# Deferred attention work behind every second score tile, and modulation rows loaded from GpSimd's queue

## The chip, the cores and the metric

The kernel runs on one core of a Trainium2 chip. The metric is the device time of one execution in microseconds (us); lower is better. A profile is one further execution, recorded by the hardware profiler. Its engines are PE (TensorE: PE is the matmul, PEld the weight load beside it), DVE (VectorE), ACT (ScalarE), POOL (GpSimd) and SP (SyncE, which here only issues transfers); SPq and POOLq are the instruction queues of SP and GpSimd. L344 is line 344 of the kernel in question.

## The reference

One block of a diffusion backbone works on 512 latent tokens and 256 context tokens of width 1024. The inputs are modulated, one combined projection feeds two kinds of attention, both are gated and merged, and a mixture of 16 experts follows. Cut to what is computed:

```python
mod = silu(c) @ w_ada + b_ada                 # w_ada: 1024 x 6144
sh1, sc1, g1, sh2, sc2, g2 = split(mod, 6)
mod_c = silu(c_ctx) @ w_ada + b_ada           # its first two parts
h, hc = x * (1 + sc1) + sh1, ctx * (1 + sc1c) + sh1c
p, pc = h @ w_in, hc @ w_in                   # 1024 x 4000
# latent attention: c_q, c_kv by rms_norm, then w_uq, w_ukv; 8 heads
o_mla = softmax(q_mla k_mla^T * scale) v_mla
# differential attention: 4 heads, two score maps each
w = softmax(q1 k1^T * s) - lam * softmax(q2 k2^T * s)
o_diff = rms_norm(w dv, g_subln) * (1 - lambda_init)
y = gate_a * (o_mla @ w_o_mla) + gate_b * (o_diff @ w_o_diff)
x = layer_norm(alpha * x + g1 * (y @ w_out))
x = layer_norm(alpha * x + g2 * ec_moe(x * (1 + sc2) + sh2))
# ec_moe: each of 16 experts takes its 64 best tokens, SwiGLU of 1024
```

The first third of the modulation, sh1 and sc1, is wanted at once, since the projections read x and ctx modulated by it. The other four parts, g1, sh2, sc2 and g2, are wanted only behind the attention.

## The kernel before

Everything up to the experts is written for a framework whose scheduler fixes, when the kernel is built, the order of the instructions on each engine; an engine then runs its own list in order, waits included. Code order counts in that, and the rings of buffers count: a tile with bufs=3 is a ring of three, and a fourth user waits until the first buffer's last reader is done.

**Start.** The parts sh1 and sc1 are worked out by quarters of the columns. For each quarter, SP loads two blocks of w_ada (tile wa, L222 and L223, 128x2048 each), a quarter of x and ctx (xq, L226 and L227), and a page of w_in (wraw, L196). PE multiplies the w_ada blocks by the activated condition (tile tp, L237), DVE copies the result (ms, L240), PE transposes it, and DVE adds it up to the scales and shifts (scv, shv). Then x is transposed on PE, modulated on DVE (xtmp), and split into a rounded part (xlh, xch on ACT) and a rest (xll, xcl on GpSimd, L78). A product of two such pairs is three matmuls (L82 to L84), into the accumulators acc. The key projection of the differential attention runs in step with the quarters.

**Projections.** chunk() and gates() go through the columns of w_in. A weight page wraw is split like x into whi (ACT, L75) and wlo (DVE, L78). There are six pages of this kind.

**Modulation rows.** The other four parts of the modulation need 32 loads of 128x1024 floats (512 KB) of w_ada, L344. DVE multiplies each by one column of the condition and adds the eight of a part up (L346 for the first of eight, L348 for the others). After eight, mod_sum() sums over the partitions on PE (L358), loads two rows of b_ada (L359) and adds them on DVE (L360) into rm. The tile is wa2 (wa in the profile), a ring of N_WA = 3 that the b_ada rows share. The calls of mod_chunk() are set by a table of places, MOD_AT: eight within the value projection, twelve in gates(0), twelve in gates(1). What the eighth row leaves to do, mod_sum(), stands in a list, late, and is run by the next call. All these loads are issued by SP, in whose queue the pages of w_in, w_ukv and w_uq stand too.

**Attention.** A score tile is one block of 128 queries against 768 keys: scores() on PE (tile sc, L653), the maximum on DVE (L642), the exponential on ACT (L643). The transposes of the weights (tpb, L661) and the value products (av, L841 in the latent attention) are put off: defer() queues them with a cost and the earliest slot, and fill() runs as many of them as a share of the queued cost allows. fill() is called after each score tile, four calls in a half head, and each counts as one slot. A value product of one 128-key block (kc) is one deferred piece of cost 0.43 (differential) or 0.86 (latent, two heads at once).

**Experts.** From about 560 us on the order is written out by hand; the weights of the experts stream through the same pages, and through others that come free behind the attention.

## Time and profile before

| | us |
|---|---|
| median of three runs | 1046.89 |
| lowest and highest of them | 1044.27 and 1050.75 |
| the profiled execution | 1044.37 |
| its span in the profile | 1042.6 |
| PE busy | 980.1 (94%) |
| DVE busy | 447.2 (43%) |
| ACT busy | 278.3 (27%) |
| POOL busy | 173.4 (17%) |
| bytes moved | 266.98 MB, mean 256 GB/s |

The span is what the profile shows of the execution; the time holds 1.77 us more around it. PE is busy nearly throughout, but a busy PE may still be at different work per microsecond, and a short wait of PE in one stage can come from an engine that is mostly idle. So the stretches have to be read one by one: start (0 to 46 us), projections (to 150), gates with latent projections and modulation rows (to 262), differential attention (to 330), latent attention (to 460), output projection and router (to 560), experts (from there).

### The profile page before, as it was taken

The page shows a single profiled execution, that of the slowest core. Times are in us where ns is not written, and L with a number is a line of the kernel's source. Part 1 is how long each engine was busy: PE and PEld are TensorE (multiplying, and loading weights), DVE is VectorE, ACT ScalarE, POOL GpSimd, SP SyncE. Part 2 cuts the span into 40 slices and gives each one's busy share as a digit, 9 for nine tenths or more (in the row PEclk, how much of TensorE's full clock was granted, in tenths as well). Part 3 has the DMA queues.
Part 4 walks back from the last instruction along what each step waited for, and adds up shares of the span by engine and source line. Part 5 has one row for each costly group of instructions (what it writes and reads, how often), then busy time and mean ns, then how long its engine had stood idle before and what let it go on. Part 6 is the DMA issues. An engine that isn't in the chain of part 4 may idle for free.

```text
span 1042.6 us, 13825 instructions
## 1 busy us (share of the span) xinstructions
PE 980.1 (94%) x5280; PEld 615.3 (59%) x5280; DVE 447.2 (43%) x871; ACT 278.3 (27%) x556; POOL 173.4 (17%) x176
## 2 busy tenths in 40 slices
PE   6999999999989999999996999999999999999982
PEld 5888977768778777777764443535353534234331
DVE  2382366662678555558473312221313131111227
ACT  1222325224777555544110101010101010010010
POOL 2340020202677322210021400000000000000004
PEclk9999999999999999999998999999999999999997
DMA  9944347752111100038948989999999999999993
GB/s 299 289 157 131 96 119 257 239 189 78 27 35 57 41 1 21 21 99 300 406 161 325 376 303 408 409 409 409 409 408 409 409 409 409 409 409 409 410 371 118
DMA packets 101210, 266.98 MB, mean 256 GB/s; under 512 B 14020, under 2 KB 37528, under 8 KB 101144
## 3 DMA queue, kind: packets, MB, share of 16 engines
q1 hardware_dynamic: 100248, 264.52, 68.2%
q0 software_dynamic: 320, 1.05, 0.3%
q8 instruction: 42, 0.69, 0.3%
q10 hardware_dynamic: 576, 0.52, 0.1%
q14 instruction: 24, 0.20, 0.1%
HBM read 261.47 MB, written 2.10 MB: 253 GB/s over the span
## 4 chain that ended last, share of the span: by engine, by line
PE 70%; DMA 10%; issue 9%; DVE 5%; POOL 2%; ACT 2%; SPq 0%; POOLq 0%; DVEq 0%; ACTq 0%
PE h L1179 15%; PE y L1195 8%; PE mx L1142 6%; PE acc L82 5%; PE acc L84 5%; PE acc L83 5%; DMA wr<-moe_w 5%; PE sc L653 4%; DMA wa<-w_ada 3%; PE tpb L661 3%; PE av L841 3%; PE mx L1208 2%; PE po L84 1%; PE po L83 1%; PE po L82 1%
## 5 line engine op out<-in xcount | busy, mean ns | idle before, releaser
L1179 PE MATMUL h<-wr,xe 128*64 128x512 f32 x1024 | 233.6, 598 | 8.9 <-DMA wr<-moe_w 7.9
L1179 PEld LDWEIGHTS h<-wr,xe 128*64 128x64 f32 x1024 | 68.2, 136 | 163.0 <-issue 106.6
L1195 PE MATMUL y<-wr,hidT 128*64 128x512 f32 x448 | 97.7, 594 | 0.0
L642 DVE TENSOR_REDUCE nm<-sc 128x1 f32<-128x768 f32 x64 | 61.0, 953 | 34.4 <-PE sc L653 33.8
L1182 DVE TENSOR_TENSOR hid<-hid,h 128x512 f32<-128x512 f32 x16 | 11.0, 688 | 147.8 <-PE h L1179 147.8
L1195 PEld LDWEIGHTS y<-wr,hidT 128*64 128x64 f32 x448 | 31.5, 137 | 61.8 <-issue 58.2
L1154 POOL TENSOR_TENSOR oh<-oh,aff 128x512 f32<-128x512 f32 x8 | 8.4, 1048 | 350.2 <-PE mx L1142 350.2
L643 ACT ACTIVATE P<-sc,nm 128x768 f32<-128x768 f32 x64 | 57.6, 901 | 31.8 <-DVE nm L642 22.7
L1142 PE MATMUL mx<-oh,xn 128*128 128x128 f32 x512 | 60.4, 280 | 1.4 <-DVE oh L1132 1.4
L1142 PEld LDWEIGHTS mx<-oh,xn 128*128 128x128 f32 x512 | 59.4, 196 | 2.5 <-issue 1.3
L75 ACT ACTIVATE whi<-wraw 128x1024 fp32r<-128x1024 f32 (+1 forms) x32 | 33.5, 1046 | 100.8 <-DMA wraw<-w_in 76.8
L78 DVE TENSOR_TENSOR wlo<-wraw,whi 128x1024 fp32r<-128x1024 f32 (+1 forms) x32 | 38.7, 1209 | 45.0 <-PE acc L83 29.1
L75 ACT ACTIVATE ye<-y 128x512 fp32r<-128x512 f32 (+2 forms) x17 | 9.7, 572 | 178.1 <-DVE y L1202 98.7
L82 PE MATMUL acc<-xlh,whi 128*128 128x512 f32 x128 | 51.6, 403 | 2.8 <-ACT whi L75 2.0
L1209 DVE TENSOR_TENSOR acc<-acc,mx 128x512 f32<-128x512 f32 x56 | 34.7, 680 | 41.4 <-PE mx L1208 41.4
L1181 ACT ACTIVATE hid<-h 128x512 f32<-128x512 f32 x16 | 9.6, 597 | 154.9 <-PE h L1179 154.9
L83 PE MATMUL acc<-xll,whi 128*128 128x512 f32 x128 | 50.8, 397 | 0.0
L82 PE MATMUL acc<-whi,xlh 128*128 128x512 f32 (+1 forms) x128 | 49.5, 391 | 1.0 <-ACT whi L75 1.0
L84 PE MATMUL acc<-xlh,wlo 128*128 128x512 f32 x128 | 50.0, 398 | 0.0
L1202 DVE SCALAR_TENSOR_TENSOR y<-y,gate,g2b 128x512 f32<-128x512 f32 x14 | 9.9, 754 | 92.6 <-PE y L1195 92.6
L84 PE MATMUL acc<-whi,xll 128*128 128x512 f32 (+1 forms) x128 | 48.7, 381 | 0.5 <-POOL xll L78 0.5
L83 PE MATMUL acc<-wlo,xlh 128*128 128x512 f32 (+1 forms) x128 | 48.8, 381 | 0.2 <-DVE wlo L78 0.2
(341 smaller groups left out, 1704.4 us busy)
## 6 DMA issues: line engine op xcount, KB each, us to landing
wr<-moe_w SPq DMA_DIRECT2D x372, 512.0 KB, 10.2
wa<-w_ada SPq DMA_DIRECT2D x32, 512.0 KB, 4.6
wraw<-w_in SPq DMA_DIRECT2D x28, 512.0 KB, 4.8
wa<-w_ada SPq DMA_DIRECT2D x8, 1024.0 KB, 9.8
wr<-moe_w SPq DMA_DIRECT2D x16, 384.0 KB, 8.4
outraw<-w_out SPq DMA_DIRECT2D x8, 512.0 KB, 11.1
xq<-x SPq DMA_DIRECT2D x4, 512.0 KB, 7.8
q<-q SPq DMA_DIRECT2D x16, 128.0 KB, 2.3
```

The source lines that it names most:

```text
L75: S.activation(hi, src, AF.Copy)
L78: (eng_lo or V).tensor_tensor(lo, src, f(hi), op=OP.subtract)
L82: T.matmul(ps, lh, rh, start=start, stop=False)
L83: T.matmul(ps, lh, rl, start=False, stop=False)
L84: T.matmul(ps, ll, rh, start=False, stop=stop)
L642: V.tensor_reduce(nm, ps[:, :768], axis=AX.X, op=OP.max, negate=True)
L643: S.activation(p, ps[:, :768], AF.Exp, bias=nm, accum_out=z)
L653: T.matmul(ps[:, a:b], l, r[:, a:b], start=i == 0, stop=i == len(passes) - 1)
L1142: T.matmul(pss[hf][:, kk * 128:(kk + 1) * 128], xn[t][:, k * 128:(k + 1) * 128], o[:, t].rearrange("p e s -> p (e s)"), start=t == 0, stop ...
L1179: T.matmul(ph[i][64 * hf:64 * hf + 64, :], xe[:, k, sl], w[:, hf * 512:(hf + 1) * 512], start=k == 0, stop=k == KD - 1)
L1195: T.matmul(py[hf][r0:r0 + 64, :], hT[:, e % 2, fc % 4, fc // 4, :], w[:, hf * 512:(hf + 1) * 512], start=fc == 0, stop=fc == KD - 1)
L1209: V.tensor_tensor(acc[t][:, hs], acc[t][:, hs], ps, op=OP.add)
```

## The change

It does three things. The modulation rows and the b_ada rows are issued by GpSimd instead of SP. mod_chunk() first issues and multiplies its own row and only then runs what the row before it left to do. In the attention, two score tiles are issued together, then their softmaxes, and fill() is called once for the two, with two slots and twice the share of the queued cost; the value products are deferred in threes (differential) or all six at once (latent).

```diff
--- before.py
+++ after.py
@@ -334,14 +334,17 @@
 
     def mod_chunk():
 
-        for fn in late:
+        due = late[:]
+        late.clear()
+        if len(halves) < 4 * KD:
+            mod_part()
+        for fn in due:
             fn()
-        late.clear()
-        if len(halves) == 4 * KD:
-            return
+
+    def mod_part():
         j, k = divmod(len(halves), KD)
         wa = mw.tile([128, D], F32, name="wa2", bufs=N_WA)
-        dma(wa, w_ada[:, k, (2 + j) * D:(3 + j) * D])
+        G.dma_start(wa, w_ada[:, k, (2 + j) * D:(3 + j) * D])
         if k == 0:
             V.tensor_scalar(wa, wa, cs[:, 0, 0:1], None, op0=OP.mult)
         else:
@@ -356,7 +359,7 @@
         bm = mw.tile([128, D], F32, name="wa2", bufs=N_WA)
         for g in (2 * h, 2 * h + 1):
             T.matmul(pm[32 * g:32 * g + 32, :], one2[:, 0:1].to_broadcast([128, 32]), wa[:, (g % 2) * 512:(g % 2) * 512 + 512], start=True, stop=True)
-            dma(bm[32 * g:32 * g + 32, :512], b_ada[4 + 4 * i + g:5 + 4 * i + g].to_broadcast([32, 512]))
+            G.dma_start(bm[32 * g:32 * g + 32, :512], b_ada[4 + 4 * i + g:5 + 4 * i + g].to_broadcast([32, 512]))
         V.tensor_tensor(rm[i][64 * h:64 * h + 64], pm[64 * h:64 * h + 64], bm[64 * h:64 * h + 64, :512], op=OP.add)
 
     def chunk(col, n, cuts, evac, at, nxt):
@@ -512,10 +515,10 @@
             first = turns[turn] = max(first, turns.get(turn, 0))
         later.append((cost, first, fn, key))
 
-    def fill(parts):
-
-        slot[0] += 1
-        budget = sum(w[0] for w in later) / parts
+    def fill(parts, n=2):
+
+        slot[0] += n
+        budget = n * sum(w[0] for w in later) / parts
         i = 0
         while i < len(later) and budget > 0:
             c, first, fn, _ = later[i]
@@ -750,14 +753,15 @@
                     prep_pair(0)
             for t in (2 * half, 2 * half + 1):
                 z1 = wk.tile([128, 1], F32, name="z1", bufs=6)
-                ps_ = []
+                ps_, scs = [], []
                 for m in range(2):
                     q1, q2, k1 = (qk[hd, m, nm] for nm in ("q1", "q2", "k1"))
                     tsl = slice(t * 128, (t + 1) * 128)
-                    sc = scores([(q1[:, tsl], k1), (q2[:, tsl], k1)])
-                    ps_.append(softmax(sc, z1 if m else z0[:, t:t + 1],
+                    scs.append(scores([(q1[:, tsl], k1), (q2[:, tsl], k1)]))
+                for m in range(2):
+                    ps_.append(softmax(scs[m], z1 if m else z0[:, t:t + 1],
                                        wpage("P1", F32, [128, D])[:, :768] if m else p_tile()))
-                    fill(D_PARTS)
+                fill(D_PARTS)
 
                 V.reciprocal(z1, z1)
                 V.scalar_tensor_tensor(z1, z1, nlam, z0[:, t:t + 1], op0=OP.mult, op1=OP.mult)
@@ -780,8 +784,8 @@
                     finish(hd, avs[hd], z0, ("d", hd))
             for j in range(3):
                 defer(0.45, lambda j=j, tr=tr: tr(j), D_TR, ("d", hd), "tr")
-            for kc in range(NK):
-                defer(0.43, lambda kc=kc, pv=pv: pv(kc), D_TR + 1, ("d", hd), "pv")
+            for k0 in range(0, NK, 3):
+                defer(1.3, lambda k0=k0, pv=pv: [pv(kc) for kc in range(k0, k0 + 3)], D_TR + 1, ("d", hd), "pv")
     close_qb()
 
     w_od = A["diff_w_o"][0].rearrange("(k p) n -> p k n", p=128)
@@ -813,18 +817,19 @@
         if h % 2 == 1 and pr + 1 < HEADS // 2:
             prep_pair(pr + 1)
         for half in range(2):
-            ws_ = []
+            ws_, scs = [], []
             for t in (2 * half, 2 * half + 1):
                 tsl = slice(t * 128, (t + 1) * 128)
                 qx, qy = qts[h][0][:96, tsl], qts[h][1][:96, tsl]
                 kx, ky = kt[h % 3][0][:96], kt[h % 3][1][:96]
-                sc = scores([(qx, kx), (qx, ky), (qy, kx)])
+                scs.append(scores([(qx, kx), (qx, ky), (qy, kx)]))
+            for sc in scs:
                 z = wk.tile([128, 1], F32, name="zm", bufs=6)
                 p = softmax(sc, z, p_tile())
                 V.reciprocal(z, z)
                 G.tensor_scalar(p, p, z, 1.0, op0=OP.mult, op1=OP.mult)
                 ws_.append(p)
-                fill(M_PARTS)
+            fill(M_PARTS)
 
             def tr(j, ws_=ws_, h=h, half=half):
                 if j == 0:
@@ -847,8 +852,7 @@
             for j in range(3):
                 defer(0.45, lambda j=j, tr=tr: tr(j), M_TR, None, "tr")
             if h % 2 == 1:
-                for kc in range(NK):
-                    defer(0.86, lambda kc=kc, pv=pv: pv(kc), M_TR + 1, None, "pv")
+                defer(2.6, lambda pv=pv: [pv(kc) for kc in range(NK)], M_TR + 1, None, "pv")
             if half == 1:
                 box = []
                 if h % 2 == 0:
```

(In the attention's lines G is GpSimd, V is DVE, T is PE and S is ACT.)

The order at three places shows what this moves. The first is GpSimd's and DVE's list at the start of the program, before against after; wa_739 and its like are modulation rows, tri is a constant mask, xll and xcl are the rests of x and ctx of the first quarter. GpSimd:

```order
 masks.py:65 MEMSET tri 128x128
+L347 DMA wa_739<-w_ada 128x1024
 masks.py:66 AFFINE_SELECT tri<-tri 128x128
+L347 DMA wa_760<-w_ada 128x1024
+L347 DMA wa_787<-w_ada 128x1024
+L347 DMA wa_808<-w_ada 128x1024
+L347 DMA wa_835<-w_ada 128x1024
 L78 TENSOR_TENSOR xll<-xtmp,xlh 128x512
 L78 TENSOR_TENSOR xcl<-xtmp,xch 128x256
 L78 TENSOR_TENSOR xll<-xtmp,xlh 128x512
 L78 TENSOR_TENSOR xcl<-xtmp,xch 128x256
+L347 DMA wa_856<-w_ada 128x1024
```

Five row loads now stand ahead of the first quarter's rests on GpSimd, and the next behind them. DVE, at the same place, where cs is the condition's columns and vecs a table of biases:

```order
 L169 TENSOR_SCALAR cs<-sg 128x8
+L349 TENSOR_SCALAR wa_739<-wa_739,cs 128x1024
+L351 SCALAR_TENSOR_TENSOR wa_760<-wa_760,cs,wa_739 128x1024
 L240 COPY ms<-tp 128x128
 L183 COPY vecs<-tp 128x68
+L351 SCALAR_TENSOR_TENSOR wa_787<-wa_787,cs,wa_760 128x1024
 L184 TENSOR_SCALAR gsub<-vecs 128x1
 L247 SCALAR_TENSOR_TENSOR scv<-tp,vecs 128x4
```

Two multiplications by rows that are still to be loaded stand ahead of the copy ms of the first quarter, and a third ahead of scv.

The second place is the stretch of gates(0) and the latent projections. SP's list before, where wraw is a page of w_in and wa2 a modulation row:

```order
L196 DMA wraw_1439<-w_in 128x2x512
L344 DMA wa2_1382<-w_ada 128x1024
L344 DMA wa2_1397<-w_ada 128x1024
L196 DMA wraw_1485<-w_in 128x2x512
L344 DMA wa2_1412<-w_ada 128x1024
L344 DMA wa2_1421<-w_ada 128x1024
L466 DMA wukv_1530<-mla_w_ukv 128x1024
L471 DMA wuq_1536<-mla_w_uq 128x768
L344 DMA wa2_1436<-w_ada 128x1024
L344 DMA wa2_1451<-w_ada 128x1024
L471 DMA wuq_1540<-mla_w_uq 128x768
L196 DMA wraw_1740<-w_in 128x2x512
```

SP's list of the change at this place:

```order
L196 DMA wraw_1439<-w_in 128x2x512
L196 DMA wraw_1485<-w_in 128x2x512
L469 DMA wukv_1530<-mla_w_ukv 128x1024
L474 DMA wuq_1536<-mla_w_uq 128x768
L474 DMA wuq_1540<-mla_w_uq 128x768
L196 DMA wraw_1740<-w_in 128x2x512
L196 DMA wraw_1779<-w_in 128x2x512
```

The rows are gone from it, and only weight pages are left. GpSimd's list of the change there, in which qtok is the sum that closes the rotary embedding of the latent queries, and of which the list before had only the qtok lines:

```order
L347 DMA wa2_1436<-w_ada 128x1024
L347 DMA wa2_1451<-w_ada 128x1024
L347 DMA wa2_1460<-w_ada 128x1024
L347 DMA wa2_1475<-w_ada 128x1024
L362 DMA wa2_1479<-b_ada 32x512 x2
L347 DMA wa2_1497<-w_ada 128x1024
L347 DMA wa2_1506<-w_ada 128x1024
L502 TENSOR_TENSOR qtok_1334<-q1t_1601,q2t_1602 128x2x32
L502 TENSOR_TENSOR qtok_1335<-q1t_1601,q2t_1602 128x2x32
L347 DMA wa2_1521<-w_ada 128x1024
L502 TENSOR_TENSOR qtok_1336<-q1t_1619,q2t_1620 128x2x32
```

The rows now stand in line with the qtok sums, which wait for DVE.

The third place is PE in the latent attention. Its list before, where av is a value product (wT holds transposed weights, vm the values), sc a score matmul and tpb a transpose:

```order
L841 MATMUL av<-wT,vm 64x256 x11
L653 MATMUL sc<-K,Q 128x512 x3
L653 MATMUL sc<-K,Q 128x256 x3
L661 MATMUL tpb<-ident,P 128x128 x8
L841 MATMUL av<-wT_3224,vm 64x256
L661 MATMUL tpb<-ident,P 128x128 x4
L841 MATMUL av<-wT_3454,vm 64x256
L653 MATMUL sc<-K,Q 128x512 x3
L653 MATMUL sc<-K,Q 128x256 x3
L841 MATMUL av<-wT_3224,vm 64x256
L841 MATMUL av<-wT_3454,vm 64x256
L841 MATMUL av<-wT_3224,vm 64x256
```

PE's list of the change there:

```order
L664 MATMUL tpb<-ident,P 128x128 x4
L846 MATMUL av<-wT,vm 64x256 x11
L664 MATMUL tpb<-ident,P 128x128 x4
L656 MATMUL sc<-K,Q 128x512 x3
L656 MATMUL sc<-K,Q 128x256 x3
L656 MATMUL sc<-K,Q 128x512 x3
L656 MATMUL sc<-K,Q 128x256 x3
L664 MATMUL tpb<-ident,P 128x128 x8
L846 MATMUL av<-wT_3550,vm 64x256
```

The products, which before were broken up by scores and transposes, now stand in one block, and two score tiles follow each other.

## Rows read from the trace of the kernel before

**Rows 1.** Busy time by stretch, whole span.
```profile
...
core 0: us, PE busy (x) PEld busy (x) DVE busy (x) ACT busy (x) POOL busy (x), PEclk, DMA share, GB/s
2.00:46.00 44.00, 36.63 (x313) 29.89 (x314) 13.77 (x30) 9.05 (x17) 11.85 (x11) 1.00 1.02 323
...
150.00:226.00 76.00, 71.44 (x309) 55.29 (x308) 50.13 (x82) 24.52 (x63) 6.72 (x16) 0.98 0.74 245
...
262.00:330.00 68.00, 62.17 (x379) 52.49 (x377) 50.41 (x86) 50.21 (x108) 47.65 (x36) 1.00 0.14 30
330.00:460.00 130.00, 126.79 (x780) 96.04 (x782) 76.62 (x130) 71.96 (x137) 37.21 (x38) 1.00 0.13 41
...
560.00:1015.00 455.00, 444.72 (x2259) 192.03 (x2257) 108.17 (x213) 48.13 (x94) 21.97 (x20) 1.00 1.00 394
```

**Rows 2.** Who waited for whom on PE, 0 to 62 us: total, times, longest.
```profile
...
PE tp L237 <- DMA wa<-w_ada: 4.2, 2, 4.0
...
PE acc L82 <- ACT whi L75: 1.0, 1, 1.0
```

**Rows 3.** DMA issues of SP in order of time, 10 to 30 us.
```profile
...
18.37 4.46 SPq L223 DMA_DIRECT2D wa<-w_ada  x1
```

**Rows 4.** The chain of waits, whole span: start us, us, what.
```profile
...
22.82 1.94 PE tp L237 x32
...
35.46 3.22 PE tp L237 x64
...
376.77 1.24 PE sc L653 x6
...
382.73 1.05 PE sc L653 x6
...
862.52 10.18 DMA wr<-moe_w
```

**Rows 5.** Instructions on the tile wa, whole span: its loads.
```profile
...
DMA to landing us min/median/max: 2.0/4.6/14.0
```

**Rows 6.** Line 344, 150 to 228 us.
```profile
...
L344 SPq DMA_DIRECT2D wa<-w_ada x23: 327/328/350, 151.1 to 218.4; - x23
...
DMA to landing us min/median/max: 3.5/4.6/5.0
```

**Rows 7.** Line 348, 150 to 228 us: duration ns min/median/max.
```profile
...
L348 DVE SCALAR_TENSOR_TENSOR wa<-wa,cs,wa x21: 1276/1284/1337, 154.8 to 223.6; 128x1024 f32<-128x1024 f32 x21
```

**Rows 8.** The chain of waits, 150 to 232 us.
```profile
...
152.16 4.59 DMA wa<-w_ada
156.84 1.30 DVE wa L348
...
173.52 1.29 DVE wa L348
174.86 1.05 PE tp L358 x4
...
202.84 6.64 DMA wraw<-w_in
```

**Rows 9.** Who waited for whom on PE, 140 to 262 us.
```profile
...
PE acc L82 <- ACT whi L75: 2.0, 1, 2.0
PE tp L358 <- DVE wa L348: 1.5, 1, 1.5
PE acc L82 <- DVE q2t L496: 0.8, 1, 0.8
```

**Rows 10.** Busy time around one wait of PE.
```profile
...
210.70:214.60 3.90, 3.90 (x10) 3.05 (x11) 3.33 (x3) 0.41 (x1) 0.00 (x0) 0.58 0.91 285
```

**Rows 11.** GpSimd in order of time, 560 to 610 us.
```profile
...
565.61 0.76 POOL L1217 DMA_DIRECT2D gb<-ln_g  x1 [20.23 <-issue]
...
571.78 0.59 POOL L1217 DMA_DIRECT2D gb<-ln_g  x1 [1.04 <-PE h L1179]
```

**Rows 12.** Line 1217, whole span: from issue to landing.
```profile
...
DMA to landing us min/median/max: 6.1/6.5/7.8
```

## The prediction

> **What bounds the kernel now.** I read the busy time by stretch first [rows 1]. In every stretch PE is the engine nearest to full, but for two reasons. At the start transfers fill the span: 323 GB/s, and PE is busy 36.6 of 44 us. In the experts the DMA share is 1.00 at 394 GB/s. In between, PE itself is the limit: it is idle 4.6 of 76 us in the gates' stretch, 5.8 of 68 in the differential and 3.2 of 130 in the latent attention. So an edit there can win only those few idle microseconds or the cost of the order in which PE works; and it can lose as much as it makes PE wait.
>
> Then the waits of PE one by one. At the start it waits 4.2 us for wa, the blocks of w_ada, and 1.0 us for a weight page [rows 2]. Between 140 and 262 us it waits 2.0 us for whi, 1.5 us for the product of a modulation row and 0.8 us for a rotary sum [rows 9]. The 2.0 us has a page of w_in behind it that came late (wraw, 6.64 us in the chain) [rows 8], and behind it the granted clock fell to 0.58 for 3.9 us [rows 10], mostly the lower of its two levels (1.2 and 2.4 GHz), after PE had stood idle; at full speed the same work takes 0.58 x 3.9 = 2.3 us, so 1.6 us more were lost.
>
> Last the chain of waits there [rows 8]: it runs DMA wa 4.59, DVE wa 1.30, and on to the sum on PE (L358, 1.05). This is the chain of modulation rows, 23 of whose 32 loads fall between 151.1 and 218.4 us [rows 6]: with three buffers, a load can start only when a product is done. A row lands 4.6 us after its issue in the median and is multiplied in 1.28 [rows 6, 7]; 22 steps in 67.3 us are 6.1 us for two of them, and 4.6 + 1.28 is 5.9. So two rows are under way at a time, and the ring's round is a landing and a product. PE waits for that chain only 1.5 us: the chain is as long as PE's work beside it, with next to no reserve.
>
> **The modulation rows, at the start.** GpSimd's order lets it issue three row loads at once, as soon as its constants are set, and each further one when DVE has done a product; before, the first stood in SP's queue behind the whole start. The ring bounds how many can be out: three. The transfer engines are full here, so each row of 0.524 MB that comes before the quarters' last block pushes that back by 1.33 us at 394 GB/s to 1.62 at 323 [rows 1]. Nine rows stand ahead of the third quarter's copy on DVE. Four of them fall ahead of the first projection: 5.3 to 6.5 us. Nine by the third quarter would be 12 to 14.6 us, less the slack that the later quarters have: the block issued at 18.37 us [rows 3] lands at most 14.0 us later [rows 5], at 32.4, and is used at 35.46 [rows 4], so 3.1 us; that leaves 8.9 to 11.5. With seven it is 9.3 less 3.1, 6.2 us. If the ring lets through its first three alone, 4.0. I take +7: nearest to seven rows, since PE's first waits are for these very blocks [rows 2]. The range is +4 to +11.5. Two products also stand ahead of the copy ms in DVE's list, and a third ahead of scv; they cost 1.28 us each, but what can hold DVE there is their rows' landing, and behind DVE stand ms, PE's transposes, xtmp and every projection. I put that into the same term, since both wait for the same bytes. GpSimd, in turn, holds the rests of x (xll) behind its fourth and fifth row loads, which wait for products.
>
> Speaking against the whole idea of another queue is that the transfer engines have no room here (share 1.02 [rows 1]), and that an issue costs SP 0.33 us, which no one waits for [rows 6]. The Trainium skill has this as a rule, in "DMA: Bandwidth & Descriptors", section "Issuing engines are not separate DMA queues": transfers from different engines interleave on the same 16, and issuing from several saves only the time of the issue. By that rule the start's sum is as here, and the gates' stretch would gain nothing but the issues; the trace agrees with it so far as a full share can show.
>
> **The modulation rows, in the gates' stretch.** Here the wait of SP's queue for a free buffer goes, and with it what stood behind it: weight pages. That can win PE's waits of 2.0, 1.5 and 0.8 and the 1.6 us of clock, about −6 us in all [rows 9, 10]. Against it stands the landing. No row of w_ada was loaded by GpSimd before; the nearest rows are the two of the final norm's scale and shift, gb, of 256 KB, half as many bytes. GpSimd is held 0.59 to 0.76 us by the issue of one [rows 11], and it lands 6.1, 6.5 and 7.8 us after (least, median, most) [rows 12], among other transfers. SP's loads, twice the bytes, land in 3.5, 4.6 and 5.0 [rows 6]. I take the smallest of GpSimd's, 6.1, since the gates' stretch has its transfer engines busy 0.74 against 1.00 in the experts' [rows 1], where gb was loaded. That is +1.5 per round of the ring; 23 rows, two to a round, are 12 rounds: +18, less the 1 us that the late page's wait takes off: +17 on the chain, and PE waits for nearly all of it, because its sums stand in its list at fixed places among the gates' matmuls. The bounds are −6 (every wait gone, landing no longer than now) and 3.2 x 12 − 1 = +37 (landing 7.8). In GpSimd's list the rows also stand behind qtok sums that wait for DVE; in SP's list they waited for DVE as well, so I put nothing on it. Issuing the next row before the former part's sum saves one round's wait on PE in each of three parts, but the buffer that the next row wants is the one that the sum is still reading, and it waits as before: nothing.
>
> **The attention.** What moves is order alone. Six score matmuls take 1.24 us behind a product and 1.05 behind transposes [rows 4]: 0.19 us for a change of kind. The blocks of products fall from 22 to 15: −1.4 us. Two score tiles side by side save some changes more, about as many as three: −0.6. So −2. What could be late next is the softmax: with two score buffers, and DVE and ACT each 50 of 68 us busy in the differential attention [rows 1], a pair that is scored at once makes PE wait for two softmaxes before the next pair if nothing else is left to do. All the idle time gone is 9.0 us, so the bounds are −10.4 and, by doubling that idle time, +9.0.
>
> **Behind that.** The output projection, router and experts move with the end of the attention, one for one: the first weights of the experts go into pages that PE frees, and then the transfers at 394 GB/s set the time [rows 1]; where the chain of the experts waits, it is for them (10.18 us) [rows 4].
>
> **The sum.** The profiled execution took 1044.4 us, 2.5 below the median of 1046.9. 1044.4 + 7 + 17 − 2 = 1066.4; I predict 1066. A change of 1%, 10.5 us, is about what a measurement of this kernel can tell from none.
>
> **The rivals.**
>
> *Not slower: the freed queue wins.* If GpSimd's rows land in 4.6 us or less, the chain keeps its length, the weight pages come early, and PE's waits go (−6); the attention's pairs fill half its idle time (−4); the start costs its least (+4). 1044.4 + 4 − 6 − 4 = 1038. It decides at a landing of 4.6 us. For it: the gb loads came while the experts' weights filled the transfer engines, so their landing may be a queue's time and not GpSimd's. Against it: even the least of them is beyond the most of SP's [rows 6, 12]. Chance 0.07.
>
> *No difference to be told: rows land in about SP's longest time.* At 5.0 us [rows 6], +0.4 a round, 12 rounds less 1: +3.8. 1044.4 + 7 + 3.8 − 2 = 1053. For it speaks what spoke for the first; also that two loads are under way on different buffers, so that part of a longer landing could lie beside the other row's product. Against it: the ring's round already is a landing and a product, so that a longer landing shows in full. Chance 0.20. The Trainium skill, "DMA: Bandwidth & Descriptors", section "Specifications", gives about 1 us to the first byte for GpSimd's path and 0.6 for SP's, 0.4 us apart; by that alone it would come out as this rival does. The trace of before, with 6.1 against 4.6, speaks for more.
>
> *Worse.* GpSimd's queue is held by its own waits and its rows land in 7.8 us: the chain takes +37 at most, and at the start +11. I price the chain halfway between +17 and +37, since the median landing, 6.5, is nearer to the least: 1044.4 + 11 + 27 + 4 (attention not winning) = 1086. For it: one of the few GpSimd loads in the trace took that long [rows 12]. Against it: it was loaded while the transfer engines were full. Chance 0.13.
>
> *The change does not do what it says:* in the attention, that the pairs break up again. The order shows them side by side, so this can only cost the −2: no case of its own.
>
> **How the numbers follow.** The forecast, 1066 with its own range of 1056 to 1082, has 0.60; the rivals 0.07, 0.20 and 0.13. The range from 1046 to 1084 leaves out the first rival (0.07), some of the third (0.10) and little else. Faster by over 1% (below 1036) is half of the first rival: 0.03. Within 1% (up to 1057.4) are its other half, most of the second (0.18) and the lower edge of the forecast (0.04): 0.26. Slower: 0.71.
>
> **What would show it.** Landings of the row loads on GpSimd: about 6 us in the gates' stretch, and 5.9 us per pair of rows grown to 7.4; PE's wait for the product of a row (L351 after) grown from 1.5 us to over 10; the gates' stretch longer by 17 us, at a granted clock that falls where PE waits. At the start, PE's wait for wa grown by about 7 us. In the attention, PE's idle time no greater. Wrong would be: rows that land in 4 us, a gates' stretch that is shorter with no wait for wraw, or a stretch of attention that is over 5 us off.

## The result

The changed kernel takes 1065.6 us (median of four runs, 1064.93 to 1066.12), the kernel before, run beside it, 1046.2 (1044.27 to 1050.75). The ratio is 1.0168, with a 95% interval of 1.0142 to 1.0193: 19.4 us slower. The profiled execution of the change took 1065.41 us, with a span of 1063.3; that of before had 1044.37 and 1042.6.

**Where the time went.** The rows of line 82 in the two traces give the ends of the stages: `acc<-whi,xlh` starts with the first projection, `acc<-xlh,whi` starts and ends with the gates' stretch, `po<-woh,yh` starts the output projection. The columns after the form's count are the duration in ns (least, median, most), and the start of the first and of the last in us. First the kernel before, whose stage bounds the rows ahead of the prediction did not show:

```profile
L82 PE MATMUL acc<-whi,xlh x128: 346/389/504, 15.9 to 142.9; 128*128 128x512 f32 x96, 128*128 128x416 f32 x32
L82 PE MATMUL acc<-xlh,whi x128: 387/389/628, 144.4 to 261.7; 128*128 128x512 f32 x128
L82 PE MATMUL po<-woh,yh x64: 387/394/500, 483.6 to 538.1; 128*128 128x512 f32 x64
```

The same rows of the change:

```profile
L82 PE MATMUL acc<-whi,xlh x128: 346/389/776, 20.8 to 151.0; 128*128 128x512 f32 x96, 128*128 128x416 f32 x32
L82 PE MATMUL acc<-xlh,whi x128: 388/389/628, 152.5 to 279.5; 128*128 128x512 f32 x128
L82 PE MATMUL po<-woh,yh x64: 387/392/503, 501.2 to 555.6; 128*128 128x512 f32 x64
```

| stretch | before | change | difference | forecast |
|---|---|---|---|---|
| start and projections, to the first gates' matmul | 144.4 | 152.5 | +8.1 | +7 |
| gates, latent projections and rows, first to last L82 | 117.3 | 127.0 | +9.7 | +17 |
| both attentions, to the first of the output projection | 221.9 | 221.7 | −0.2 | −2 |
| from there to the end of the span | 559.0 | 562.1 | +3.1 | 0 |

The last line is no work of the change: in the profiled executions of the experiments below, which leave that part alone, the same stretch takes 559.0 to 563.0 us, and the kernel before has one of the two shortest. The other three lines are what there is to explain.

**The start.** PE's waits in the first 62 us (total, times, longest, in us), of the change, answering to [rows 2]:

```profile
PE tp L237 <- DMA wa<-w_ada: 7.5, 2, 7.1
...
PE tp L258 <- issue: 2.4, 1, 2.4
PE tp L258 <- DVE shv L250: 0.8, 1, 0.8
```

PE waits 3.3 us more for the blocks of w_ada, and two waits are new. The view names DVE for the shorter one only; DVE's timeline shows that the longer one, which ends at 35.10, stands behind it as well. DVE adds up shv, which frees the buffer that PE's transpose needs, behind a product that waited 4.05 us for its row (start, duration, in us; in brackets the idle time before it and what ended it):

```profile
33.57 1.29 DVE L351 SCALAR_TENSOR_TENSOR wa<-wa,cs,wa 128x1024 f32<-128x1024 f32 x1 [4.05 <-DMA wa<-w_ada]
...
34.84 0.15 DVE L250 TENSOR_TENSOR shv<-tp,vecs 128x4 f32<-128x4 f32 x1
```

The first accumulating matmul starts at 20.8 us instead of 15.9. PE's lower clock has a part in the start's loss too: from 20 to 46 us the granted clock is 0.93, where it was 1.00, and 26 us at 0.93 are 1.8 us lost (columns as in [rows 1], before and change):

```profile
20.00:46.00 26.00, 25.36 (x220) 20.65 (x219) 8.54 (x16) 6.00 (x10) 6.94 (x7) 1.00 1.04 329
```

```profile
20.00:46.00 26.00, 22.61 (x188) 17.73 (x189) 13.96 (x17) 5.27 (x10) 12.90 (x14) 0.93 1.07 368
```

**The gates' stretch.** The same view from 62 to 300 us, against [rows 9]:

```profile
PE tp L361 <- DVE wa L351: 10.9, 3, 5.5
PE tpb L664 <- POOL P L769: 1.5, 1, 1.5
```

One wait is left, and it has grown from 1.5 to 10.9 us: PE stands at three sums for the last product of a part. The waits for whi (2.0) and q2t (0.8) are gone. The rows' loads in this stretch, against [rows 6]:

```profile
L347 POOL DMA_DIRECT2D wa<-w_ada x23: 537/542/606, 159.5 to 232.5; - x23
...
DMA to landing us min/median/max: 3.9/4.5/6.8
```

This is the line that the prediction did not expect: a row on GpSimd lands 4.5 us after its issue (median), where on SP it was 4.6. The issue holds the engine 0.54 us instead of 0.33, and first to last load are 73.0 us apart instead of 67.3.

What lies between a product and the load that it makes room for is seen in the timelines. GpSimd and DVE of the change:

```profile
159.52 0.61 POOL L347 DMA_DIRECT2D wa<-w_ada  x1 [4.54 <-PE tp L361]
160.54 0.54 POOL L347 DMA_DIRECT2D wa<-w_ada  x1 [0.41 <-DVE rm L363]
165.09 0.54 POOL L347 DMA_DIRECT2D wa<-w_ada  x1 [4.01 <-DVE wa L351]
```

```profile
163.51 1.28 DVE L351 SCALAR_TENSOR_TENSOR wa<-wa,cs,wa 128x1024 f32<-128x1024 f32 x1 [2.14 <-DMA wa<-w_ada]
```

The product ends at 164.79 and GpSimd issues at 165.09, 0.30 us later. On SP (here the experiment with the rows back in its queue) the product at 154.89 ends at 156.17 and the load starts at 156.20, 0.03 us later:

```profile
156.20 3.29 SPq L347 DMA_DIRECT2D wa<-w_ada  x2
...
161.49 0.33 SPq L474 DMA_DIRECT2D wuq<-mla_w_uq  x1
```

```profile
154.89 1.28 DVE L351 SCALAR_TENSOR_TENSOR wa<-wa,cs,wa 128x1024 f32<-128x1024 f32 x1 [1.45 <-DMA wa<-w_ada]
```

**Where the sums stand.** PE's order differs too; the prediction had taken the sums' places as fixed. The sums of the last three parts have 636, 744 and 832 accumulating matmuls ahead of them in the change, 644, 753 and 841 before. The queue alone moves them so; that the scheduler expects GpSimd's rows sooner is a guess. The last matmul of the last sum starts at 239.3 us, 86.8 after the stretch's beginning, against 225.6 and 81.2 before; behind it come 40.2 us of the stretch, against 36.1. So of the 9.7 us, 5.6 lie ahead of that point and 4.1 behind it.

```profile
L361 PE MATMUL tp<-wa,one x16: 592/823/1063, 158.2 to 239.3; 128*32 128x512 f32 x16
```

A sum's matmul takes 0.82 us in the median, 0.60 before: many run at the lower clock, right after PE has stood idle. By windows, the whole stretch had a granted clock of 0.99 before and has 0.95 in the change. Before:

```profile
144.40:261.70 117.30, 112.26 (x518) 88.14 (x516) 67.20 (x113) 41.26 (x93) 15.76 (x26) 0.99 0.57 185
```

The change:

```profile
152.50:279.50 127.00, 115.96 (x519) 90.62 (x518) 67.25 (x113) 41.66 (x93) 32.55 (x55) 0.95 0.52 171
...
290.00:300.00 10.00, 8.53 (x41) 7.43 (x39) 5.59 (x11) 5.80 (x13) 6.35 (x5) 0.83 0.00 0
```

So of the 9.7 us, 6.0 are more idle time of PE (11.0 against 5.0), and 3.7 are the same work taking longer (116.0 against 112.3 busy). The last line is in the differential attention: 10 us at 0.83 are 1.7 us lost there. In the runs below with the attention alone, with the rows on SP and with the first nine there, that stretch is at 1.00 throughout.

### The profile page after: what moved, and what is told of

The parts are those of the page before. It is cut to its first block, busy times and chain, and to the rows that moved or that the text cites. A ratio compares the mean times of both kernels' runs of the same rounds, so it can differ in the third digit from the quotient of the medians.

```text
span 1063.3 us, 13836 instructions
## 1 busy us (share of the span) xinstructions
PE 988.3 (93%) x5280; PEld 622.1 (59%) x5280; DVE 443.6 (42%) x871; ACT 278.0 (26%) x556; POOL 193.4 (18%) x216
## 4 chain that ended last, share of the span: by engine, by line
PE 70%; issue 11%; DMA 10%; DVE 4%; POOL 2%; ACT 2%; SPq 0%; POOLq 0%; DVEq 0%; ACTq 0%
PE h L1183 15%; PE y L1199 8%; PE mx L1146 6%; PE acc L84 5%; PE acc L83 5%; DMA wr<-moe_w 5%; PE sc L656 5%; PE acc L82 5%; DMA wa<-w_ada 4%; PE tpb L664 3%; PE av L846 2%; PE mx L1212 2%; PE av L781 2%; PE po L84 1%; PE po L83 1%
## 5 line engine op out<-in xcount | busy, mean ns | idle before, releaser
L82 PE MATMUL acc<-xlh,whi 128*128 128x512 f32 x128 | 51.3, 401 | 0.0
L1185 ACT ACTIVATE hid<-h 128x512 f32<-128x512 f32 x16 | 9.6, 597 | 155.5 <-PE h L1183 155.5
L82 PE MATMUL acc<-whi,xlh 128*128 128x512 f32 (+1 forms) x128 | 49.7, 392 | 0.5 <-ACT xlh L75 0.5
L351 DVE SCALAR_TENSOR_TENSOR wa<-wa,cs,wa 128x1024 f32<-128x1024 f32 x28 | 36.5, 1305 | 31.4 <-DMA wa<-w_ada 31.2
```

The source lines that it names most:

```text
L82: T.matmul(ps, lh, rh, start=start, stop=False)
L351: V.scalar_tensor_tensor(wa, wa, cs[:, k, 0:1], halves[-1], op0=OP.mult, op1=OP.add)
```

## The experiments

The stretches below are, as in the table above, from the start of the first to that of the last L82 matmul of a stage; in the expectations, the gates' stretch is counted to the last matmul's end and is 0.6 to 0.9 us longer for that. Ratios are to the kernel before, run beside it on the same chip. Each stretch is read from one profiled execution. How far it varies by itself is seen where the loads are those of before: the gates' stretch takes 117.3 us before and 119.8 with the attention alone.

**The attention alone.** The kernel before with the change's lines of the attention; in mod_chunk() and mod_sum() nothing is changed.

```diff
-        due = late[:]
-        late.clear()
-        if len(halves) < 4 * KD:
-            mod_part()
-        for fn in due:
+        for fn in late:
             fn()
+        late.clear()
...
-        G.dma_start(wa, w_ada[:, k, (2 + j) * D:(3 + j) * D])
+        dma(wa, w_ada[:, k, (2 + j) * D:(3 + j) * D])
...
```

> The kernel before with the attention's part of the change alone (pairs of score tiles, products in blocks, one fill for two tiles); rows and b_ada stay in SP's queue and in the old order. Theory: the change's 19 us are all made ahead of the attention (8.1 at the start, 9.6 in the gates' stretch by the two traces), so this kernel is within 2 us of the kernel before (1044 to 1048), with PE's idle time of 9.0 us in both attentions moved by less than 1. Rival: the blocks win their 1.4 to 2 us of changes and the trace of the change hid it behind a shifted start: 1044 or less, and a stretch from the first score to the last product shorter by 2 us.

1046.96 us against 1048.94; the ratio is 0.9978 (0.9962 to 0.9994), 2 us faster. From the last gates' matmul to the output projection it takes 220.1 us, against 221.9 before. So by the stretch the rival held, and the change's own trace hides the gain; the time itself lies in the theory's range. The gain recurs: with the old attention the stretch takes 221.9 to 223.4 us in three traces, with the new one 220.0 to 221.8 in all others. It is busy time of PE and not waiting, as the windows of the whole stretch show, first before, then with the attention alone (PE idle 9.0 and 9.3 us):

```profile
261.70:483.60 221.90, 212.87 (x1263) 167.38 (x1262) 145.41 (x240) 132.64 (x258) 84.86 (x74) 1.00 0.19 59
```

```profile
264.00:484.10 220.10, 210.81 (x1263) 167.24 (x1262) 141.76 (x240) 131.50 (x258) 83.87 (x74) 1.00 0.19 59
```

Which of the two attentions wins it, the value products' rows do not say:

```profile
L843 PE MATMUL av<-wT,vm x192: 378/379/432, 365.3 to 461.3; 128*64 128x256 f32 x192
L778 PE MATMUL av<-wT,dv x96: 377/379/402, 278.0 to 350.2; 128*128 128x256 f32 x96
```

From the last gates' matmul (264.0) to the last differential product (350.2) are 86.2 us, 88.3 before (261.7 to 350.0); from there to the last latent product 111.1, before 110.7. But the order moves work across that boundary. Before, 120 transposes of weights stand ahead of the last differential product, here 96:

```profile
L661 PE MATMUL tpb<-ident,P x120: 270/272/332, 270.8 to 349.7; 128*128 128x128 f32 x120
```

```profile
L661 PE MATMUL tpb<-ident,P x96: 270/273/329, 273.0 to 346.7; 128*128 128x128 f32 x96
```

Four more in a row take 0.44 us (eight 1.04, four 0.60), so the 24 are some 2.6 us, no less than the 2.1. In the change the first figure is 87.8: 1.6 of the 2.1 us went to the spell at the lower clock.

**The rows back on SP.** The change, with only the queue undone:

```diff
-        G.dma_start(wa, w_ada[:, k, (2 + j) * D:(3 + j) * D])
+        dma(wa, w_ada[:, k, (2 + j) * D:(3 + j) * D])
...
-            G.dma_start(bm[32 * g:32 * g + 32, :512], b_ada[4 + 4 * i + g:5 + 4 * i + g].to_broadcast([32, 512]))
+            dma(bm[32 * g:32 * g + 32, :512], b_ada[4 + 4 * i + g:5 + 4 * i + g].to_broadcast([32, 512]))
```

> The changed kernel with the modulation rows and the b_ada rows back in SP's queue; the new order of mod_chunk (next row ahead of the part's sum) and the attention stay. Theory A (the queue did it): start back to that of before (-8), gates' stretch back to within 2 us of before, so 1046 to 1049. Theory B (the new order did the gates' stretch, since the b_ada pair now gets its buffer one row later and the ring waits for the sum's addition): the start is back, but 4 to 9 us of the gates' stretch stay, so 1050 to 1055, with the waits of row loads for the addition (9.1 us in the change) still there.

1047.98 us, ratio 0.9984 (0.9963 to 1.0004). Theory A held: the start is back (the gates begin at 144.6 us), the gates' stretch takes 118.2, and what is left is the attention's gain. The new order of mod_chunk() costs nothing on SP. So the whole loss is the queue's.

**The queue alone.** The kernel before with both loads on GpSimd (the two lines above the other way round, in the old order of mod_chunk()).

> The kernel before with the rows and the b_ada rows issued by GpSimd, in the old order of mod_chunk, and the old attention. GpSimd's list has the same row loads at the start as the change, and PE's list has the sums as early as in the change (636, 744 and 832 accumulating matmuls ahead of the last three, against 644, 753 and 841 before). Theory A: start +8 and the whole +9.6 of the gates' stretch, 1063 to 1066. Theory B: start +8, and in the gates' stretch only the 4 us of matmuls that now stand behind the last sum, and the 0.28 us by which GpSimd issues later behind a product, 1057 to 1061.

1075.08 us, ratio 1.024 (1.0215 to 1.0264): worse than either theory, and than the change. The gates begin at 159.9 us, 15.5 later than before, and take 128.4 (+11.1). In the old order the first part's b_ada rows come ahead of the ninth row, in the start as well; PE now waits for DVE's copies there, which stand in line behind a row's product:

```profile
PE tp L237 <- DMA wa<-w_ada: 7.2, 2, 6.7
PE tp L245 <- DVE ms L240: 4.3, 2, 4.1
```

So the new order is a help to the queue, not a cost: against this kernel the change saves 7.4 us of the start (some of it lower clock: 0.97 here from 46 us to the gates, 1.00 in the change). The 1.4 us of the gates' stretch are less than that stretch varies by itself. Both theories fell.

**The first nine rows on SP, the rest on GpSimd.**

```diff
-        G.dma_start(wa, w_ada[:, k, (2 + j) * D:(3 + j) * D])
+        (dma if len(halves) < 9 else G.dma_start)(wa, w_ada[:, k, (2 + j) * D:(3 + j) * D])
```

> The changed kernel with its first nine row loads back in SP's queue, where they stand behind the whole start; the other 23 and the b_ada rows stay on GpSimd. Theory: the start's +8.1 us are the bytes of these nine rows ahead of the quarters' blocks, so they go and nothing else does: 1056 to 1059, first accumulating matmul at 15.9 us as before, and the gates' stretch as in the change (+9 to +10). Rival: the start is late for another reason (GpSimd's rests of x behind its own queue, or DVE's copies behind products), which here goes as well; then the times are the same, but the blocks of w_ada would land in the change as early as before, which its trace does not show (PE waits 7.1 us for the first, 4.0 before).

1057.8 us, ratio 1.008 (1.0053 to 1.0106). The gates begin at 144.7 us: the start's loss is the nine early rows and nothing else. The gates' stretch keeps its own, 126.2 us, and PE's wait for the sums is 10.6. The attention takes 220.1 here, with its gain.

**Half of the bytes at the start.**

```diff
-        G.dma_start(wa, w_ada[:, k, (2 + j) * D:(3 + j) * D])
+        n = 512 if j == 0 else D
+        G.dma_start(wa[:, :n], w_ada[:, k, (2 + j) * D:(2 + j) * D + n])
...
-            V.scalar_tensor_tensor(wa, wa, cs[:, k, 0:1], halves[-1], op0=OP.mult, op1=OP.add)
+            V.scalar_tensor_tensor(wa[:, :n], wa[:, :n], cs[:, k, 0:1], halves[-1][:, :n], op0=OP.mult, op1=OP.add)
```

> The changed kernel in which the eight rows of the first part are loaded and multiplied in their first 512 columns alone, and both sums of that part read those columns: half of that part's modulation is left out. At the start 2.1 MB less go ahead of the quarters' blocks, in the same order on GpSimd. Theory: the start's +8.1 us are bytes, so about half of them go (2.1 MB at 323 to 394 GB/s are 5.3 to 6.5 us): start +2 to +4 instead of +8.1, and the time 4 to 6 us under the change's, 1060 to 1062. Rival: the start is late because DVE and GpSimd stand in line behind rows whose landing has a floor that bytes don't set; then at most 2 us go: 1063 to 1066.

1065.87 us, ratio 1.0152 (1.0118 to 1.0187). 2.1 MB less, and the gates begin at 154.2 us, later still than in the change (152.5). The rows land 6.0 us after their issue (median), in the change 7.2: half the bytes take nearly as long. PE's wait for w_ada falls from 7.5 to 5.6 us, but it now waits 4.2 for DVE's copy ms. In DVE's list three products, not two, stand ahead of the first copy here, which the shorter products bring with them; so this run does not change the bytes alone. And the granted clock is 0.87 from 20 to 46 us, where the change has 0.93: 1.6 us more are lost to it. The rival's time held.

```profile
PE tp L237 <- DMA wa<-w_ada: 5.6, 1, 5.6
PE tp L245 <- DVE ms L240: 4.2, 2, 4.0
```

**Next to no bytes.** The same with n = 32, and the first part's sum reading the 32 columns again and again.

```diff
-        n = 512 if j == 0 else D
+        n = 32 if j == 0 else D
```

> The changed kernel in which the eight rows of the first part are loaded and multiplied in 32 columns alone (16 KB instead of 512), and that part's sum repeats those columns: nearly all of that part's modulation is left out. Only the ninth row still comes whole ahead of the start's last blocks. With half rows the start did not get shorter. Theory (line): what makes the start late is that DVE's copies and additions for the quarters stand in line behind products that wait for a row, and GpSimd's rests of x behind row loads; a landing that takes 4 to 6 us whatever its size then still leaves the projections' end 4 us or more later than before: 1060 or more. Rival (bytes): with the bytes gone the landings become short, and the projections end within 2 us of before (145 to 147 us for the first matmul of the gates, 152.8 in the change): 1056 to 1059.

1061.66 us, ratio 1.0127 (1.0102 to 1.0153). The gates begin at 148.1 us: 4.4 of the 8.1 us go, 3.7 stay. The first accumulating matmul is at 16.4 us, nearly as early as before; what stays is later, with a wait of 2.4 us for wlo, DVE's half of the weights' split:

```profile
PE tp L237 <- DMA wa<-w_ada: 4.2, 1, 4.2
...
PE acc L83 <- DVE wlo L78: 2.4, 1, 2.4
```

DVE's timeline has the product of a row, which waited for its landing, right ahead of wlo:

```profile
19.06 0.25 DVE L352 SCALAR_TENSOR_TENSOR wa<-wa,cs,wa 128x32 f32<-128x32 f32 x1 [1.99 <-DMA wa<-w_ada]
19.23 1.22 DVE L78 TENSOR_TENSOR wlo<-wraw,whi 128x1024 fp32r<-128x1024 f32 x1
```

Behind that wait the granted clock is 0.93 from 20 to 46 us (before 1.00), some 1.8 us. A 16 KB load still lands only 2.3 to 6.6 us after its issue, 5.7 in the median. So the rival fell, and the line's time held: about half of the 8.1 us are the bytes, and the half that stays is a wait in DVE's list (2.1 us more idle time of PE) and the lower clock that follows it. One whole row and the b_ada pair are left in this run, so the share of the line is rather smaller.

**Only the b_ada rows on SP.** The change, with the one line of mod_sum() back on SP.

> The changed kernel with only the b_ada rows back in SP's queue; the w_ada rows stay on GpSimd. The last two sums now stand later in PE's list (750 and 845 accumulating matmuls ahead of them, against 744 and 832; the second at 636 as in the change). Theory (place): what the gates' stretch lost is that PE's sums stand too early for the chain, so that DVE's next products and PE's matmuls wait for each other; with the sums later, 4 to 7 of the 9.6 us go: 1058 to 1062. Rival (issue): each row costs GpSimd 0.28 us more between a product and the next load, some 3.4 us for 12 rounds, and the ring does the rest; then the chain's length from its first load to its last product stays at 78 to 79 us and at most 2 us go: 1063 to 1066.

1062.78 us, ratio 1.0132 (1.0101 to 1.0163). The gates' stretch takes 126.4 us instead of 127.0, although the last sum has 13 matmuls more ahead of it. It comes at 242.6 us, 89.7 after the stretch's beginning, where the change has 86.8. The time lies between the two forecasts, nearer to the rival's. Putting the sum later in the list moved the sum, not the end; but the chain of rows got longer too, 81.8 us from its first load to its last product where the rival had 78 to 79, so the place was not moved alone. The rest of the difference to the change is in the attention, 220.1, at full clock here.

**Releasing SP's loads over GpSimd.** The kernel with the rows on SP, and in the gates' stretch a small clearing of each buffer on GpSimd ahead of its load.

```diff
+        if len(halves) > 8:
+            G.memset(wa[:, :64], 0.0)
         dma(wa, w_ada[:, k, (2 + j) * D:(3 + j) * D])
```

> The kernel with all rows on SP, new order and new attention, in which GpSimd first clears 64 columns of each row's buffer in the gates' stretch; SP's load waits for that. So each load is released over GpSimd, but goes over SP's queue; the sums stand in PE's list as with SP alone (645, 753, 845). Theory (release): the gates' stretch is as long as it is on GpSimd because each load starts later behind the product that frees its buffer, by 0.28 us there, and 12 rounds add that up; here the delay is 0.3 to 0.6 us, so the gates' stretch grows by 4 to 7 us, from 118.8 to 123 to 126, and the time to 1051 to 1055. Rival (reserve): SP's chain has room for it, and what GpSimd loses comes from elsewhere: at most +2, 1047 to 1050.

1047.27 us, ratio 0.9991 (0.9974 to 1.0008), against 0.9984 without the clearing. The rival held, in time and stretch. The product below ends at 156.33 and SP issues at 156.57, 0.24 us later, the median here; without the clearing it was 0.03.

```profile
155.05 1.28 DVE L353 SCALAR_TENSOR_TENSOR wa<-wa,cs,wa 128x1024 f32<-128x1024 f32 x1 [1.61 <-DMA wa<-w_ada]
```

```profile
156.57 2.87 SPq L349 DMA_DIRECT2D wa<-w_ada  x2
```

The gates' stretch takes 120.0 us, 1.8 more than without the clearing, but only 0.2 more than with the attention alone (119.8), which has no such delay: the 1.8 are not clear of how the stretch varies, and PE's idle time in it did not grow (5.8 us, 5.6 without). Its loads, though, are now as far apart as GpSimd's: 72.4 us from first to last, against 66.1 without the clearing, 69.7 with the attention alone, and 73.1 with 23 rows on GpSimd.

```profile
L349 SPq DMA_DIRECT2D wa<-w_ada x23: 327/328/350, 151.5 to 223.9; - x23
```

```profile
PE tp L363 <- DVE wa L353: 2.9, 2, 2.2
```

So the late release can stretch the chain of loads, and that alone does not make PE wait: 2.9 us for the sums here, 10.6 on GpSimd, whose last three sums stand 9, 9 and 13 matmuls earlier in PE's list. That points to the sums' places; no run moves them alone.

**A longer delay, and later sums.** The kernel with its first nine rows on SP and the rest on GpSimd, where GpSimd also clears 512 columns of each later buffer first.

```diff
+        if len(halves) > 8:
+            G.memset(wa[:, :512], 0.0)
         (dma if len(halves) < 9 else G.dma_start)(wa, w_ada[:, k, (2 + j) * D:(3 + j) * D])
```

> The changed kernel with its first nine row loads on SP (the gates' stretch is 126.7 us in that one, 117.9 before), in which GpSimd also clears 512 columns of each later row's buffer ahead of its load. That makes every load later, by what the clearing takes, and the scheduler, which counts it, now puts the sums later in PE's list: 645, 760 and 857 accumulating matmuls ahead of the last three, against 636, 744 and 832, and 644, 753 and 841 before. Theory (place): the larger part of what GpSimd costs in the gates' stretch is that PE stands early at sums whose rows are late, at once idle and then at the lower clock, while DVE's work waits for PE; with the sums later the stretch gets shorter by 3 us or more although each load is later: 123.5 or less, and PE's wait for the sums falls from 10.6 to under 7. Rival (chain): the chain of rows alone sets the stretch, wherever the sums stand; it gets longer by 12 times the clearing's time, 3 to 6 us: 129 or more.

1061.57 us, ratio 1.0117 (1.0076 to 1.0157). The place theory's forecast failed: the gates' stretch takes 132.6 us, 6.4 more than without the clearing (126.2), and PE waits 15.0 us for its sums though they stand 9 to 25 matmuls later. A load now starts 0.88 us after its product (median; the one below after a product that ended at 158.33), 0.58 more than without the clearing; 12 rounds of that are 7.0, and first to last load are 83.3 us apart instead of 73.1. The agreement with the 6.4 is loose: 4.2 of them are idle time of PE and 2.2 its lower clock, and the medians of the two kernels are only 3.8 us apart. Since each load came later as well, the run does not show what the places alone are worth.

```profile
158.40 0.53 POOL L348 MEMSET wa<- 128x512 f32 x1 [4.51 <-DVE wa L353]
159.22 0.54 POOL L349 DMA_DIRECT2D wa<-w_ada  x1 [0.30 <-POOL wa L348]
```

```profile
L349 POOL DMA_DIRECT2D wa<-w_ada x23: 537/540/606, 151.9 to 235.2; - x23
```

```profile
PE tp L363 <- DVE wa L353: 15.0, 3, 8.1
```

**Three attempts at a faster version**, all with the loads on SP. First, a buffer of its own for the b_ada rows:

```diff
-        bm = mw.tile([128, D], F32, name="wa2", bufs=N_WA)
+        bm = up.tile([128, 512], F32, name="bm", bufs=1)
...
```

> The kernel before with a buffer of its own for the b_ada rows, so that they don't take one of the ring's three; all loads on SP. PE's list now has the sums much earlier: 600, 726 and 805 accumulating matmuls ahead of the last three, against 644, 753 and 841. Theory (place): PE waits longer for each sum, over 8 us in all against 1.5, and the kernel is slower by 2 to 8 us, although the chain itself has a buffer more. Rival (chain): a free ring makes the chain shorter and the place costs nothing: 1040 to 1044.

1051.19 us, ratio 1.0022 (1.0004 to 1.0039). The gates' stretch falls to 111.4 us, but it begins at 154.5: with a buffer free, eight more rows move into the projections, and DVE's split of the weights stands behind their products. PE, which never waited there, waits 6.1 us for wlo:

```profile
PE acc L83 <- DVE wlo L78: 6.1, 4, 4.6
PE tp L358 <- DVE wa L348: 1.7, 1, 1.7
```

Neither theory was right: PE's wait for the sums hardly grew, and the loss came in a stage that neither spoke of.

Second, the calls placed earlier, with the new attention:

```diff
-MOD_AT = ((1, 4), (), (), (0, 1, 3), (0, 1, 3))
+MOD_AT = ((1, 4), (1, 4), (1, 3), (3,), (3,))
```

> The kernel before with the attention's part of the change, and 24 of the 32 calls of mod_chunk placed in the projections (eight in each of three), where the transfer engines are 0.42 busy; eight stay in the gates. All loads on SP. If the chain of rows is what the gates' stretch waits for, its PE waits (1.5 + 2.0 + 0.8) and the 1.6 us at the lower clock go: 1039 to 1043, faster than both kernels. Rival: PE's sums now stand among the projections, too early for the chain there, and PE, which is busy there throughout, waits for them instead: 1047 to 1055.

1052.28 us, ratio 1.0022 (1.0001 to 1.0042). The same again: the gates' stretch takes 111.7 us, 5.6 less than before, but begins at 155.5, 11.1 later. In the projections PE waits 4.1 us for wlo, and not for the sums, so the rival's time came by another way; in the gates' stretch it waits 2.3 for the latent norm on DVE and 1.0 for wlo.

Third, an own buffer for the last three parts alone, with the new attention:

```diff
-        bm = mw.tile([128, D], F32, name="wa2", bufs=N_WA)
+        bm = up.tile([128, 512], F32, name="bm", bufs=1) if j else mw.tile([128, D], F32, name="wa2", bufs=N_WA)
```

> The kernel before with the attention's part of the change, all loads on SP, and a buffer of its own for the b_ada rows of the last three parts; the first part's keep their place in the ring, so that no more rows are pulled into the projections, which is what made the other kernel with an own buffer slower there. The first three sums stand as before (549, 644, 753), the last earlier (810). Theory: the chain no longer waits for an addition to free a buffer at each part's end, some 1 to 2 us in each, and PE waits less: gates' stretch 115 to 118 us instead of 117.9 to 120, and the time 1 to 5 us under that of the attention's part alone (0.998 of before): 0.993 to 0.997. Rival: PE's last sum, 33 to 43 matmuls earlier, takes what the chain gains: 0.997 to 1.000.

1049.88 us, ratio 1.0011 (0.9992 to 1.003), above both forecasts. The projections keep their time (the gates begin at 144.8), but the gates' stretch takes 122.2 us. The wait for the sums stays at 1.6, and PE waits 5.6 us at once for a page of w_in, which SP issues at 209.31 us, behind two row loads that wait for products; before, the page of that place was issued at 202.84.

```profile
PE acc L82 <- ACT whi L75: 5.6, 1, 5.6
PE tp L358 <- DVE wa L348: 1.6, 1, 1.6
```

The lowest ratio is thus that of the attention's part alone, 0.9978; the two with the rows on SP, the new order and the new attention (0.9984 and 0.9991) are not told apart from it.

## Why the prediction came out, and where it did not

**The sum.** Forecast 1066, measured 1065.6. That it came out so close is luck. It was made against a profiled execution 2.5 us under its median, so that a forecast difference of 22 us stands against 19.4 measured. In the profiled executions, a term that was 7.3 us too large is made up by a start 1.1 longer, an attention whose gain did not show (1.8), and 3.1 us behind the attention that are no work of the change.

**The start: +7 forecast, +8.1 measured.** The place was right: with the nine rows back behind the start, all 8.1 us go. The reason was half right. The term was worked out as bytes ahead of full transfer engines; with nearly all of them taken away 3.7 us stay, and with half of them nothing was won. What it had named beside them, and put into the same term, counts by itself: DVE's work for the quarters stands in line behind products that wait for a landing. The lower clock that follows PE's waits, 1.8 us of the change's start, was in no term.

**The gates' stretch: +17 forecast, +9.7 measured.** This is the step that failed in its size: "the smallest of GpSimd's, 6.1", +1.5 a round. The rows land in 4.5 us. The nearest row in the trace, the 256 KB loads of gb, was taken at a DMA share of 1.00, and it was most likely the share that made it long (gb at a lower share was not tried): in the start of the change, at a share of 1.04, the rows on GpSimd land in 7.2 us (median of nine), in the gates' stretch at 0.64 in 4.5. The prediction had this as the argument for its first rival, and weighed it too low. That rival's condition, a landing of at most 4.6 us, even came true, and its result did not, because the landing is not all that the queue changes.

What took its place. The way of it was as forecast: a ring whose rounds grow, and a PE that waits for it, 10.9 us at three sums. In all PE is idle 6.0 us more in the stretch, and the lower clock makes its same work 3.7 us longer. What the queue adds to the rounds is shown in part only. GpSimd begins a load 0.30 us after its product, SP 0.03, and 12 rounds of that are 3.2 us. A release held back on purpose does move the loads apart, but what it costs the stretch is not clear of its variation: 120.0 us with SP's loads held back to 0.24, 119.8 without. So 6 us between that run and GpSimd's loads (126.2) are not settled. 1.9 of them lie ahead of the last sum and 4.3 behind it, where PE has 13 accumulating matmuls more to do. Candidates are the sums' places in PE's list, the issue that holds GpSimd 0.54 us where SP is held 0.33, and the b_ada pair that goes through the same queue (back on SP, it gave 0.6 us). Later sums did not shorten the stretch in the two runs that had them, but in one the b_ada pair was moved as well and in the other each load came later, so the places are not ruled out.

**What the freed queue was to win.** The waits for whi and q2t did go, 2.8 us, as the bound of −6 had counted; the clock did not come back but was lost more often, where PE now stands idle longer: 0.95 in the stretch against 0.99.

**The attention: −2 forecast.** Right in size, and not seen in the change's own trace: alone it is 1.8 us in the stretch and 0.9978 in the time. It is busy time of PE, with its idle time unchanged, as a cost of changing between kinds of work would show; how much of it the counted blocks are, the runs do not show.

**The rule on queues.** By the Trainium skill's "DMA: Bandwidth & Descriptors", section "Issuing engines are not separate DMA queues", another queue saves only the time of the issue. With the rows on SP or on GpSimd their median landing is 4.1 to 4.8 us in the gates' stretch; the trace agrees. The same page of the Trainium skill, section "Specifications", has GpSimd's first byte 0.4 us later than SP's. Here the landing counted from the issue shows no such difference, and what is later is the issue itself.

## What to carry to other kernels

A load's price in another queue is three things to be read apart: how long after its release it is issued, how long the issue holds the engine, and how long it lands; the last went here with how full the transfer engines were at that moment, so take it from a row at the same share. In a small ring a delay between a buffer's release and its next load comes back in every round, and a small instruction put there shows it; whether the kernel pays for it depends on whether the engine behind the ring stands waiting. Compare a difference of a stretch with what that stretch varies by itself. A load that a scheduler can move earlier takes its consumer along: in a list that runs in order, the consumer's wait then holds whatever stands behind it, and in the change's start and in the two attempts that brought rows into the projections that was work that PE needed.

## What the runs showed of the hardware that was not expected

A load of 128x1024 floats issued by GpSimd landed as soon after its issue as one issued by SP: 4.5 against 4.6 us in the median, at shares of 0.64 and 0.74. GpSimd needed 0.54 us for the issue, SP 0.33, and GpSimd began 0.30 us after the product that it waited for, SP 0.03.

A load's landing hardly follows its size at a full start: 512 KB in 7.2 us, 256 KB in 6.0, 16 KB in 5.7 (medians of nine on GpSimd's queue, the ninth always a whole row).

The lower clock came in spells that outlasted the wait: in the change and in the run with the long clearing, the differential attention had a stretch below full clock although PE did the same work there as in the runs without it; the queue alone and the own buffer for b_ada had one there too, with the old attention. What sets that off was not tried.
